# Who reads a shared PSUM bank, and in which order: opening, gates and last token tiles of a transformer layer

## The chip, the cores and the metric

The kernel runs on one core of one Trainium2 chip. The core has a matrix engine (TensorE, PE in the profile, with its weight loads as PEld), VectorE (DVE), ScalarE (ACT), GpSimd (POOL) and SyncE (SP, which here issues most of the transfers). Data move by DMA from HBM into the on-chip memory SBUF; TensorE writes its sums to PSUM, eight banks of 512 float32 columns on 128 partitions, and DVE and ACT read them there. The metric is the device time of one execution, in microseconds.

## The reference

One layer of a diffusion backbone on 512 tokens of width 1024, with 256 context tokens, batch 1, float32. What matters here:

```python
hc = modulate(rms_norm(ctx, norm1_g), sh1c, sc1c)     # sh, sc: from silu(c) @ w_ada + b_ada
s_f, s_b = context_states(hc, w_in, ...)              # k, v, gates of the context only
hx = modulate(rms_norm(x, norm1_g), sh1x, sc1x)
y_x = token_mixer(hx, ..., s_f, s_b)                  # hx @ w_in, then SGU and GLA branches, w_o
x = x + g1x * y_x
hx2 = modulate(rms_norm(x, norm2_g), sh2x, sc2x)
x = x + g2x * conv_ffn(hx2, ...)                      # 1024 -> 2 x 2816, 3x3 conv, gelu, -> 1024
return rms_norm(x, final_norm_g)
```

The token mixer's second branch is a gated linear attention (GLA) with 4 heads and two directions. Its gates are, for each direction d and head,

```python
z  = lr @ w2[d] + b2[d]                # lr: 16 columns of hx @ w_in for each direction
la = log_sigmoid(z) / 16               # computed as min(z, 0) - log(1 + exp(-|z|)), over 16
b  = cumsum(la) in chunks of 64        # then exp(b), exp(-b), exp(b_last - b) scale q and k
```

The same gates are needed for the 512 latent tokens (called x here) and for the 256 context tokens (called c).

## The kernel before

Every large product is computed as three matmuls of rounded pieces: an operand is split into a high part (a rounded copy) and a low part (the operand minus that copy), and high by high, low by high and high by low are added up in one PSUM bank. So every weight and activation costs, beside its matmuls, one cast (mostly on ACT) and one subtraction (mostly on DVE).

**Order.** The kernel is written for one core as a straight program. A scheduler that knows the tiles places semaphores between the engines; each engine then works off its instructions in the order of the program, unless a helper fixes another one. `in_order(start, engines)` chains all instructions since `start` on the engines named in the order in which they are written; it covers the opening on TensorE, ACT and DVE (from STRICT to the end of the first keys). `behind(start, name)` puts what was issued since `start` behind a named instruction. Accesses of two engines to one PSUM bank are kept apart by a semaphore, two reads too, so that the later one in program order waits for the earlier one.

**PSUM.** `mm()` and `gl()` hand out banks from two pools (mostly mm for the large products and gl for small ones); a bank asked for again waits until its last reader is done.

**Opening.** The 512 tokens are normalised, and TensorE transposes them (L585) into one bank for each block k of 128 model columns: `xps[0]` to `xps[6]` and `ps7`. `x_out` copies a bank to SBUF as xT (L590). `ada_dot(g)` computes shift and scale of a group of blocks from w_ada (tile wa, L621), DVE copies the sum to asb (L595 for the first, L768 for the rest), `ada_sel` turns it into columns (L630, L633 to L635) and `ada_mod` applies them (L642, L644) and splits the block into hxh and hxl (L374, L375). Meanwhile the loop over k adds up six banks `fps`: query and key of head 0 (gl, two banks) and the values of heads 0 and 1 for four token tiles (mm, four banks), three passes z for each k (L697). Their weights come by DMA in four pieces; `first_split(i)` splits piece i into qkh and wh on ACT (L607) and qkl and wl on DVE (L608). The dictionary `AT` says ahead of which pass z the next group's `ada_dot` stands; its `ada_sel` and `ada_mod` stand one pass later.

**Values.** After the loop each of the four value banks holds 128 tokens by 256 columns of head 0 and of head 1. `v_out` reads each half twice: ACT writes the high part (L716), DVE the low part (L717), half by half. Right behind it stand the keys of head 1 (L382) with the transposes of the context (L655, into a gl bank that ACT scales to hcf, L664).

**Heads.** Each head's gates are made by `step_z`: `step_zx` computes z of the 512 latent tokens, one bank for each direction, and `step_zc` that of the 256 context tokens, both directions in one bank of 256 columns each (L826). Of each half ACT takes the absolute value into lc (L832) and DVE the minimum with zero into mc (L833). ACT exp and ln follow (L834, L835), then DVE's running sums (`bc` for x at L875, `suf` for c at L840 and L845), and the products with q and k (L899 to L903), which TensorE transposes (L919, L927). Steps of one head run among the matmuls of other work (L401, L382) and of the head before it: L907 is the three-piece product of its outputs and states, into gl banks that DVE copies (o, L989) and ACT squares and sums (junk, L991).

**End.** The last layer product is the down projection (L1639). Token tiles 0 to 3 are finished one after the other; for each, `out_step` multiplies by the gate (yt, L1686), adds (x, L1687) and lets ACT square and sum (L1692); `out_tok` then makes the root (n3b, L1705 to L1708; ACT Sqrt, L1709; DVE reciprocal n3r, L1710), scales one half on ACT (xg, L1713, whose DMA ACT issues at L1714) and the other on DVE (L1715, whose DMA SP issues at L1716). The last tile's half is computed as 384 and 128 columns. ACT's Sqrt lies in another table of functions than what ran before; its load appears as ACT_TABLE_LOAD.

Of the kernel before, what the change touches and what calls it, by code (L numbers as in the profile page):

```python
# [16 lines left out]
P = 128  # L17
D = 1024
S = 512
LC = 256  # L20
# [13 lines left out]
def backbone_kernel(  # L34
# [58 lines left out]
    def behind(start, name):  # L93
        for i in traced()[start:]:
            tc.add_manual_dep(i, name, mybir.DependencyInfo(
                mybir.DependencyClass.NoSync, mybir.DependencyReason.DATA), reason="behind")

    ident = const([P, P], "ident")
# [505 lines left out]

    def first_split(i):
        for raw, wh, wl in (fqk[i], fv[i]):
            A.copy(wh, raw)  # L607
            V.tensor_tensor(wl, raw, wh.bitcast(F32), op=ALU.subtract)  # L608
# [28 lines left out]
    def ada_mod(g):  # L637
        k0 = G0[g]
        for k in range(k0, k0 + GROUPS[g]):
            f = fx[k]  # L640
            if k == 0:
                A.activation(f, xps[0], AF.Identity, bias=bm_[:, 0, 0:1], scale=am[:, 0, 0:1])  # L642
            else:
                V.tensor_scalar(f, f, am[:, k, 0:1], bm_[:, k, 0:1], op0=ALU.mult, op1=ALU.add)  # L644
            hx.append(split_act(f, S, "hx", eng=V.tensor_copy if k == k0 else A.copy))
            if k in (4, 6):
                first_split(k // 2)

# [60 lines left out]

    def v_out(t, ps):  # L710
        for h in range(2):
            dst = heads[h]["vx"][t // 2] if t < 4 else heads[h]["vc"]
            split_ps(*(z[:, t % 2, :] for z in dst), ps[:, h * 256:(h + 1) * 256])

    def split_ps(hi, lo, ps):
        A.copy(hi, ps)  # L716
        V.tensor_tensor(lo, ps, hi.bitcast(F32), op=ALU.subtract)  # L717
# [22 lines left out]
    x_out(2, xps[2], V.tensor_copy)  # L740
    first_split(0)
    x_out(3, xps[3], A.copy)
    x_out(4, xps[4], A.copy)
    x_out(5, xps[5], A.copy)
    x_out(6, xps[6], V.tensor_copy)
    ps7 = gl()
    for t in range(4):
        x_turn(ps7, t, KT - 1)
    x_out(KT - 1, ps7, A.copy)
    lrx = heap([96, S], F32R, s="lrx")  # L750
    fps = [gl() for _ in range(2)] + [mm() for _ in range(4)]
    AT = {0: 1, 1: 0, 2: 0, 3: 1, 4: 0}
    for k in range(KT):
        g = max(i for i in range(NG) if G0[i] <= k)
        nxt = g + 1 if k == G0[g] + GROUPS[g] - 1 and g + 1 < NG else None
        if k == 1:
            first_split(1)
        if k == 6:
# [6 lines left out]
        for z in range(3):  # L765
# [3 lines left out]
            if nxt and z == AT[g] + 1:  # L769
                ada_sel(nxt, dst)  # L770
                ada_mod(nxt)
            for i in range(6):
                if k or i > 1:
# [46 lines left out]

    def step_zc(h):
        S_ = heads[h]
        bcol, wz = gate_col(h)
# [6 lines left out]
        for d in range(2):  # L830
            zd = zc[:, d * LC:(d + 1) * LC]
            A.activation(l[:, d, :], zd, AF.Abs, bias=bcol[d])  # L832
            V.tensor_scalar(m[:, d, :], zd, bcol[d], 0.0, op0=ALU.add, op1=ALU.min)  # L833
        A.activation(l, l, AF.Exp, scale=-1.0)  # L834
# [14 lines left out]

    def step_zx(h):  # L850
        S_ = heads[h]
        bcol, wz = gate_col(h)
# [6 lines left out]
        for d in range(2):  # L859
# [4 lines left out]
            lx.append(l_)  # L864
            mx.append(m_)
        for t_ in lx:
            A.activation(t_, t_, AF.Exp, scale=-1.0)
# [3 lines left out]
        for d in range(2):  # L871
# [19 lines left out]
            S_["eq"].append(lx[d])  # L891
            S_["ek"].append(bc)
    def step_decay(h):
        S_ = heads[h]
# [14 lines left out]
    def step_z(h):  # L909
        step_zx(h)  # L910
        step_zc(h)
        step_decay(h)
# [785 lines left out]

    def out_tok(t, hf, part, before):

        b_, r = small(1, "n3b"), small(1, "n3r")
        start = len(traced())
        part()
        if before > 1:
# [4 lines left out]
        A.activation(r, ss3[:, t, before:before + 1], AF.Sqrt, bias=b_, scale=1.0 / D)  # L1709
        V.reciprocal(r, r)  # L1710
        in_order(start, V.engine)
        o = 1 - hf
        A.mul(xg[t], xg[t], r)  # L1713
        adma(out[0, t * P:(t + 1) * P, o * 512:(o + 1) * 512], xg[t])  # L1714
        V.scalar_tensor_tensor(x1[t][hf], x1[t][hf], r, fng[hf], op0=ALU.mult, op1=ALU.mult)  # L1715
        dma(out[0, t * P:(t + 1) * P, hf * 512:(hf + 1) * 512], x1[t][hf])  # L1716
# [61 lines left out]
    steps_r(r0, "p5")  # L1778
    steps_r(r1, "p5")
    for t in range(2):  # L1780
        first_half(c22[t], 1, 2 + t)
# [9 lines left out]
    for t in range(2):  # L1791
        for name, act, j in (("p1", "a12", 0), ("p5", "s4", 1)):
            for n_, i in enumerate(rbs):
                down(bank[name][t], ops[act, TAIL + n_], t, tw[i], j, False, True, again=True)
            if j == 0:
                first_half(bank[name][t], 0, t)
        out_tok(t, 1, lambda: out_step(bank["p5"][t], 1, t, 0, 512, 1), 1)
    for i, jj, p in t4s:
        down(bank["p7"][0], ops["a22", p], 0, tw[i], jj, False, True, again=True)
    out_tok(2, 0, lambda: out_step(bank["p7"][0], 0, 2, 0, 512, 1), 1)  # L1800
    for n_, (c0, n) in enumerate(((0, 384), (384, 128))):
        ps = mm()
        for i, jj, p in t4s:
            down(ps[:, :n], ops["a22", p], 1, tw[i], jj, p == TAIL, p == NP - 1, c0, n)
        step = lambda: out_step(ps[:, :n], 0, 3, c0, n, 1 + n_)
        if n_ == 0:
            step()
        else:
            out_tok(3, 0, step, 2)

# [29 lines left out]
```

## Time and profile before

| | |
|---|---|
| median of 3 runs | 929.21 us (928.75 to 931.22) |
| the profiled execution, its own time | 928.0 us |
| its span in the profile | 926.3 us |
| granted TensorE clock, mean | 0.997 |
| busy: PE, DVE, ACT, POOL | 900.1, 755.5, 483.8, 61.9 us |
| HBM read, written | 131.32 MB, 2.10 MB |

The profile is one execution; its time is 1.7 us above its span, and 1.2 us below the median. A row of the waits names the engine and line that waited, then the engine, tile and line that released it, and then the time in total, the number of such waits and the longest. A row of the timeline has the start and the duration of an instruction (or of several of one kind in a row, with their count), its line, operation, output and inputs, and in brackets how long the engine was idle ahead of it and what ended that.

### The profile page before, as it was taken

How to read it: one execution, taken by the hardware profiler on the slowest of the kernel's cores; microseconds unless marked ns; L12 is line 12 of the kernel's file. 1: busy time of each engine (PE TensorE's matmuls, PEld its weight loads, DVE VectorE, ACT ScalarE, POOL GpSimd, SP SyncE). 2: the span in 40 equal slices, each digit the busy share in tenths (PEclk: the TensorE clock that was granted, in tenths of full speed). 3: DMA queues.
4: the chain of work that ended last, by engine and by line, in shares of the span. 5: the costliest groups of instructions: out<-in, count | busy, mean ns of one | idle time of the engine just before them, and what ended most of it. 6: DMA issues, size and time to landing. Idle time of an engine off the chain costs nothing.

```text
span 926.3 us, 12858 instructions
## 1 busy us (share of the span) xinstructions
PE 900.1 (97%) x4671; PEld 754.7 (81%) x4671; DVE 755.5 (82%) x1312; ACT 483.8 (52%) x872; POOL 61.9 (7%) x90
## 2 busy tenths in 40 slices
PE   6999999999999999999999999999999999999996
PEld 5676898988878888888888877988888888888885
DVE  5567758689679878878686787899988888899997
ACT  5136546457465456757562459633333333357674
POOL 3000000000000011111111010000000000122100
PEclk9999999999999999999999999999999999999998
DMA  9940411132069474968668075344434333489632
GB/s 276 339 130 27 133 47 46 46 101 59 23 206 317 133 184 124 301 152 230 181 192 227 10 182 159 92 148 118 143 114 126 103 91 105 101 215 246 177 100 91
DMA packets 125820, 134.26 MB, mean 145 GB/s; under 512 B 7177, under 2 KB 84309, under 8 KB 125757
## 3 DMA queue, kind: packets, MB, share of 16 engines
q1 hardware_dynamic: 115357, 116.80, 40.5%
q0 software_dynamic: 8672, 15.43, 10.2%
q10 hardware_dynamic: 1728, 1.22, 0.4%
q8 instruction: 37, 0.61, 0.3%
q14 instruction: 26, 0.21, 0.1%
HBM read 131.32 MB, written 2.10 MB: 144 GB/s over the span
## 4 chain that ended last, share of the span: by engine, by line
PE 87%; DVE 5%; ACT 2%; DMA 2%; SPq 1%; issue 1%; DVEq 0%; ACTq 0%; POOLq 0%
PE mm L382 32%; PE mm L408 9%; PE gl L455 9%; PE mm L455 7%; PE gl L1639 6%; PE mm L1639 5%; PE gl L408 4%; PE gl L907 3%; PE mm L401 3%; PE mm L697 1%; PE mm L1011 1%; PE mm L393 1%; DVE bc L875 1%; SPq L319 1%; PE gl L938 1%
## 5 line engine op out<-in xcount | busy, mean ns | idle before, releaser
L143 ACT CAST wh<-raw 128x1024 fp32r<-128x1024 f32 x110 | 115.1, 1049 | 89.6 <-PE mm L382 56.5
L144 DVE TENSOR_TENSOR wl<-raw,wh 128x1024 fp32r<-128x1024 f32 x110 | 133.7, 1218 | 30.3 <-ACT wh L143 28.1
L382 PE MATMUL mm<-h2l,wh 128*128 128x512 f32 (+1 forms) x352 | 133.7, 380 | 0.0
L382 PE MATMUL mm<-h2h,wl 128*128 128x512 f32 (+1 forms) x352 | 133.6, 379 | 0.0
L382 PE MATMUL mm<-h2h,wh 128*128 128x512 f32 (+1 forms) x352 | 133.6, 379 | 0.0
L1532 DVE SCALAR_TENSOR_TENSOR cacc<-ca,ccol,cacc 128x441 f32<-128x441 f32 (+2 forms) x176 | 121.5, 693 | 4.4 <-ACT cacc L1520 0.9
L382 PEld LDWEIGHTS mm<-h2l,wh 128*128 128x128 f32 x352 | 66.2, 188 | 12.6
L382 PEld LDWEIGHTS mm<-h2h,wh 128*128 128x128 f32 x352 | 66.2, 188 | 12.5
L382 PEld LDWEIGHTS mm<-h2h,wl 128*128 128x128 f32 x352 | 66.2, 188 | 12.4
L1535 ACT ACTIVATE cacc<-cacc 128x512 f32<-128x512 f32 x22 | 13.9, 632 | 90.0 <-DVE cacc L1532 89.9
L1160 DVE SCALAR_TENSOR_TENSOR acc<-wa,cs,acc 128x512 f32<-128x512 f32 x64 | 45.5, 745 | 3.9 <-DMA wa<-in_w_ada_dram 3.9
L382 PE MATMUL mm<-hxh,wh 128*128 128x512 f32 x104 | 41.7, 401 | 0.0
L382 PE MATMUL mm<-hxh,wl 128*128 128x512 f32 x104 | 40.9, 394 | 0.0
L382 PE MATMUL mm<-hxl,wh 128*128 128x512 f32 x104 | 40.7, 392 | 0.0
L217 ACT CAST wh<-tt 128x512 fp32r<-128x512 f32 x48 | 28.4, 622 | 19.0 <-DMA tt<-in_w_in_dram 7.2
L218 DVE TENSOR_TENSOR wl<-tt,wh 128x512 fp32r<-128x512 f32 x48 | 31.7, 685 | 7.5 <-ACT wh L217 7.4
L1581 ACT CAST wh<-raw 128x1024 fp32r<-128x1024 f32 x22 | 23.0, 1052 | 17.6 <-PE mm L1639 8.5
L193 POOL DMA_DIRECT2D tt<-in_w_in_dram x24 | 20.8, 1086 | 165.8 <-DVE xl L1261 72.4
L1582 DVE TENSOR_TENSOR wl<-raw,wh 128x1024 fp32r<-128x1024 f32 x22 | 26.8, 1218 | 1.8 <-ACT wh L1581 1.7
L455 PE MATMUL mm<-wl,hxh 128*128 128x512 f32 x72 | 28.1, 391 | 0.0
L455 PE MATMUL mm<-wh,hxh 128*128 128x512 f32 x72 | 28.0, 389 | 0.0
L455 PE MATMUL mm<-wh,hxl 128*128 128x512 f32 x72 | 28.0, 389 | 0.0
(524 smaller groups left out, 2382.7 us busy)
## 6 DMA issues: line engine op xcount, KB each, us to landing
raw<-in_w_in_dram SPq DMA_DIRECT2D x54, 512.0 KB, 4.7
wa<-in_w_ada_dram SPq DMA_DIRECT2D x96, 256.0 KB, 5.1
raw<-in_ffn_w_up_dram SPq DMA_DIRECT2D x44, 512.0 KB, 4.2
raw<-in_ffn_w_down_dram SPq DMA_DIRECT2D x22, 512.0 KB, 3.5
tt<-in_w_in_dram POOLq DMA_DIRECT2D x24, 256.0 KB, 6.7
raw<-in_w_br_a_dram SPq DMA_DIRECT2D x8, 512.0 KB, 4.9
raw<-in_w_br_b_dram SPq DMA_DIRECT2D x8, 512.0 KB, 4.2
raw<-in_w_o_dram SPq DMA_DIRECT2D x8, 512.0 KB, 5.7
```

What stands on the lines that cost most here:

```text
L143: A.copy(wh, raw)
L144: V.tensor_tensor(wl, raw, wh.bitcast(F32), op=ALU.subtract)
L217: A.copy(wh[:, kk, :], tt[j][kk])
L218: V.tensor_tensor(wl[:, kk, :], tt[j][kk], wh[:, kk, :].bitcast(F32), op=ALU.subtract)
L382: T.matmul(ps, a[:, k, :], b[:, c0:c0 + n], start=(k == 0 and i == 0), stop=(k == KT - 1 and i == 2))
L401: T.matmul(ps, a[:, t * P:(t + 1) * P], b[:, k % 4, :], start=(k == 0 and i == 0), stop=(k == KT - 1 and i == 2))
L408: T.matmul(ps, a, b[:, k % 2, :], start=(k == 0 and i == 0), stop=(k == KT - 1 and i == 2))
L455: T.matmul(ps[t], a, b[:, kk, :], start=(first and i == 0), stop=(j == 1 and kk == 1 and i == 2), skip_group_check=again)
L907: T.matmul(ps, p_, q_, start=(start and z == 0), stop=(stop and z == 2))
L1160: V.scalar_tensor_tensor(a_, w_, cs[:, k, 0:1], a_, op0=ALU.mult, op1=ALU.add)
L1532: V.scalar_tensor_tensor(o, a_[:, r0 + dy:r1 + dy, c0 + dx:c1 + dx], wcol(tap), o, op0=ALU.mult, op1=ALU.add)
L1639: T.matmul(ps, a[:, t * P:(t + 1) * P], w[b][:, j, c0:c0 + n], start=(first and i == 0), stop=(last and i == 2), skip_group_check=again)
```

## The change

Five places are written in another way. What is computed stays the same; no product, copy or transfer is added or taken away.

1. Opening: `first_split` is cut into `first_high` (ACT) and `first_low` (DVE). `first_low(0)` stands behind the copies of blocks 6 and 7, and block 6 (DVE) and 7 (ACT) are copied ahead of block 5; `ps7` comes from the mm pool; `first_low(1)` stands behind `ada_mod` of block 2; and the `ada_dot` of the next group during block 2 moves from pass 0 to pass 1.
2. Values: `v_out` has both high parts of a bank on ACT first, then both low parts on DVE.
3. Gates: `step_z` has the heads of x and c (matmuls, Abs, minimum) first and then their tails; in the context's head both Abs come first and then both minima.
4. End: the root, the first and the last half of each tile are separate functions, and from tile 1 on all DVE and ACT instructions keep the order in which they are written.
5. ACT's table for Sqrt is loaded after the preparation of the last down operands, by a `preload_act_table`.

```diff
+    def table_for(func):
+        name = [i.name for i in traced() if i.engine == nc.scalar.engine][-1]
+        start = len(traced())
+        A.preload_act_table(func)
+        behind(start, name)
...
     def v_out(t, ps):
+        dst = [[z[:, t % 2, :] for z in (heads[h]["vx"][t // 2] if t < 4 else heads[h]["vc"])] for h in range(2)]
         for h in range(2):
-            dst = heads[h]["vx"][t // 2] if t < 4 else heads[h]["vc"]
-            split_ps(*(z[:, t % 2, :] for z in dst), ps[:, h * 256:(h + 1) * 256])
+            A.copy(dst[h][0], ps[:, h * 256:(h + 1) * 256])
+        for h in range(2):
+            V.tensor_tensor(dst[h][1], ps[:, h * 256:(h + 1) * 256], dst[h][0].bitcast(F32), op=ALU.subtract)
...
     x_out(2, xps[2], V.tensor_copy)
-    first_split(0)
+    first_high(0)
     x_out(3, xps[3], A.copy)
     x_out(4, xps[4], A.copy)
-    x_out(5, xps[5], A.copy)
-    x_out(6, xps[6], V.tensor_copy)
-    ps7 = gl()
+    ps7 = mm()
     for t in range(4):
         x_turn(ps7, t, KT - 1)
     x_out(KT - 1, ps7, A.copy)
+    x_out(6, xps[6], V.tensor_copy)
+    first_low(0)
+    x_out(5, xps[5], A.copy)
...
-    AT = {0: 1, 1: 0, 2: 0, 3: 1, 4: 0}
+    AT = {0: 1, 1: 0, 2: 1, 3: 1, 4: 0}
...
         if k == 1:
-            first_split(1)
+            first_high(1)
...
                 ada_mod(nxt)
+                if k == 1:
+                    first_low(1)
...
         for d in range(2):
-            zd = zc[:, d * LC:(d + 1) * LC]
-            A.activation(l[:, d, :], zd, AF.Abs, bias=bcol[d])
-            V.tensor_scalar(m[:, d, :], zd, bcol[d], 0.0, op0=ALU.add, op1=ALU.min)
+            A.activation(l[:, d, :], zc[:, d * LC:(d + 1) * LC], AF.Abs, bias=bcol[d])
+        for d in range(2):
+            V.tensor_scalar(m[:, d, :], zc[:, d * LC:(d + 1) * LC], bcol[d], 0.0, op0=ALU.add, op1=ALU.min)
...
     def step_z(h):
-        step_zx(h)
-        step_zc(h)
+        zx_head(h)
+        zc_head(h)
+        zx_tail(h)
+        zc_tail(h)
         step_decay(h)
...
+    table_for(AF.Sqrt)
...
-        out_tok(t, 1, lambda: out_step(bank["p5"][t], 1, t, 0, 512, 1), 1)
+        start = len(traced())
+        out_step(bank["p5"][t], 1, t, 0, 512, 1)
+        out_root(t, 1)
+        V.reciprocal(root[t], root[t])
+        if t == 0:
+            out_first(t, 1)
+            out_last(t, 1)
     for i, jj, p in t4s:
         down(bank["p7"][0], ops["a22", p], 0, tw[i], jj, False, True, again=True)
-    out_tok(2, 0, lambda: out_step(bank["p7"][0], 0, 2, 0, 512, 1), 1)
+    out_step(bank["p7"][0], 0, 2, 0, 512, 1)
+    out_root(2, 1)
+    out_first(1, 1)
     for n_, (c0, n) in enumerate(((0, 384), (384, 128))):
...
-        step = lambda: out_step(ps[:, :n], 0, 3, c0, n, 1 + n_)
-        if n_ == 0:
-            step()
-        else:
-            out_tok(3, 0, step, 2)
+        out_step(ps[:, :n], 0, 3, c0, n, 1 + n_)
+    out_last(1, 1)
+    V.reciprocal(root[2], root[2])
+    out_root(3, 2)
+    out_first(2, 0)
+    out_last(2, 0)
+    V.reciprocal(root[3], root[3])
+    out_first(3, 0)
+    out_last(3, 0)
+    in_order(start, V.engine, A.engine)
```

On three places the order of instructions moves as follows (line numbers of each kernel's own file; a name's number tells one tile from another).

DVE in the opening, from the split of block 0 to the split of block 1, before:

```order
L375 TENSOR_TENSOR hxl_417<-xT_270,hxh_416 128x512
L590 COPY xT_272<-mm_265 128x512
L608 TENSOR_TENSOR qkl_140<-qkraw_136,qkh_139 128x512
L608 TENSOR_TENSOR wl_115<-raw_113,wh_114 128x1024
L590 COPY xT_276<-gl_269 128x512
L768 COPY asb_467<-gl_450 128x128
L633 TENSOR_TENSOR am<-gl_473,bsc_256 128x2
...
L375 TENSOR_TENSOR hxl_480<-xT_271,hxh_479 128x512
L608 TENSOR_TENSOR qkl_162<-qkraw_158,qkh_161 128x512
L608 TENSOR_TENSOR wl_118<-raw_116,wh_117 128x1024
L768 COPY asb_510<-gl_493 128x128
```

The same stretch in the changed kernel:

```order
L381 TENSOR_TENSOR hxl_417<-xT_270,hxh_416 128x512
L596 COPY xT_272<-mm_265 128x512
L596 COPY xT_276<-gl_269 128x512
L617 TENSOR_TENSOR qkl_140<-qkraw_136,qkh_139 128x512
L617 TENSOR_TENSOR wl_115<-raw_113,wh_114 128x1024
L781 COPY asb_467<-gl_450 128x128
L642 TENSOR_TENSOR am<-gl_473,bsc_256 128x2
...
L381 TENSOR_TENSOR hxl_480<-xT_271,hxh_479 128x512
L781 COPY asb_508<-gl_491 128x128
L642 TENSOR_TENSOR am<-gl_516,bsc_256 128x2
```

The copy of block 6 (xT_276) went ahead of the low parts of piece 0, and the copy of block 2's sums (asb) no longer stands behind the low parts of piece 1.

DVE around the gates of head 1, from the copies of head 0's outputs to the products with q and k, before:

```order
L989 COPY o_1102<-gl_1581 128x256
L875 SCALAR_TENSOR_TENSOR bc_1464<-mx_1454,lx_1452 128x128 x4
L875 SCALAR_TENSOR_TENSOR bc_1477<-mx_1458,lx_1456 128x128
L879 TENSOR_TENSOR dec_1469<-bc_1464 128x4
...
L875 SCALAR_TENSOR_TENSOR bc_1477<-mx_1458,lx_1456 128x128 x3
L833 TENSOR_SCALAR mc_1494<-gl_1490,vec_b 128x256
...
L833 TENSOR_SCALAR mc_1494<-gl_1490,vec_b 128x256
...
L903 TENSOR_TENSOR lc_1493<-lc_1493,kc_1128 128x512
L989 COPY o_1101<-gl_1621 128x256
```

The same stretch in the changed kernel:

```order
L1025 COPY o_1102<-gl_1581 128x256
L729 TENSOR_TENSOR vx_1406<-mm_1594,vx_1405 128x256
L1025 COPY o_1101<-gl_1621 128x256
L852 TENSOR_SCALAR mc_1464<-gl_1460,vec_b 128x256 x2
L908 SCALAR_TENSOR_TENSOR bc_1473<-mx_1454,lx_1452 128x128 x4
L908 SCALAR_TENSOR_TENSOR bc_1486<-mx_1458,lx_1456 128x128
L912 TENSOR_TENSOR dec_1478<-bc_1473 128x4
...
L908 SCALAR_TENSOR_TENSOR bc_1486<-mx_1458,lx_1456 128x128 x3
...
L937 TENSOR_TENSOR lc_1463<-lc_1463,kc_1128 128x512
```

Both minima of the context (mc), one low part of the values and one copy of an output now stand ahead of the running sums (bc, printed as SCALAR_TENSOR_TENSOR).

DVE at the end, from tile 1's sum to tile 2's root, before:

```order
L1687 TENSOR_TENSOR x_1154_5486<-x_1154_5486,yt_8785 128x512
L1708 TENSOR_SCALAR n3b_8783<-ss_7837 128x1
L1686 TENSOR_TENSOR yt_8807<-mm_7842,g_1439_7391 128x512
L1687 TENSOR_TENSOR x_1155_5488<-x_1155_5488,yt_8807 128x512
L1710 RECIPROCAL n3r_8784<-n3r_8784 128x1
L1708 TENSOR_SCALAR n3b_8805<-ss_7837 128x1
```

The same stretch in the changed kernel:

```order
L1723 TENSOR_TENSOR x_1154_5486<-x_1154_5486,yt_8784 128x512
L1744 TENSOR_SCALAR n3b_8788<-ss_7837 128x1
L1839 RECIPROCAL n3r_8789<-n3r_8789 128x1
L1722 TENSOR_TENSOR yt_8802<-mm_7842,g_1439_7391 128x512
L1723 TENSOR_TENSOR x_1155_5488<-x_1155_5488,yt_8802 128x512
L1744 TENSOR_SCALAR n3b_8806<-ss_7837 128x1
```

Tile 1's reciprocal (n3r) now stands ahead of the two steps of tile 2 (yt and x). In the values the order on each engine is the old one; what moved there are the semaphores between ACT and DVE.

More of the change, by code (lines that the diff above doesn't have):

```diff
@@ L603, in backbone_kernel, with first_high, first_low @@
     am, bm_ = const([P, KT, 2], "am"), const([P, KT, 2], "bm")
-    def first_split(i):
+    def first_high(i):
+        for raw, wh, _ in (fqk[i], fv[i]):
+            A.copy(wh, raw)
+    def first_low(i):
         for raw, wh, wl in (fqk[i], fv[i]):
-            A.copy(wh, raw)
             V.tensor_tensor(wl, raw, wh.bitcast(F32), op=ALU.subtract)
@@ L646, in ada_mod @@
             if k in (4, 6):
-                first_split(k // 2)
+                first_high(k // 2)
+                first_low(k // 2)
     def ctx_turn(k2):
@@ L821, in step_zc, with zc_head @@
     def step_zc(h):
+        zc_head(h)
+        zc_tail(h)
+    def zc_head(h):
         S_ = heads[h]
@@ L830, in step_zc, with zc_tail @@
         for d in range(2):
-            zd = zc[:, d * LC:(d + 1) * LC]
-            A.activation(l[:, d, :], zd, AF.Abs, bias=bcol[d])
-            V.tensor_scalar(m[:, d, :], zd, bcol[d], 0.0, op0=ALU.add, op1=ALU.min)
+            A.activation(l[:, d, :], zc[:, d * LC:(d + 1) * LC], AF.Abs, bias=bcol[d])
+        for d in range(2):
+            V.tensor_scalar(m[:, d, :], zc[:, d * LC:(d + 1) * LC], bcol[d], 0.0, op0=ALU.add, op1=ALU.min)
+        S_["zc"] = l, m
+    def zc_tail(h):
+        S_ = heads[h]
+        l, m = S_.pop("zc")
         A.activation(l, l, AF.Exp, scale=-1.0)
@@ L850, in step_zx, with zx_head @@
     def step_zx(h):
+        zx_head(h)
+        zx_tail(h)
+    def zx_head(h):
         S_ = heads[h]
@@ L865, in step_zx, with zx_tail @@
             mx.append(m_)
+        S_["zx"] = lx, mx
+    def zx_tail(h):
+        S_ = heads[h]
+        lx, mx = S_.pop("zx")
         for t_ in lx:
@@ L909, in step_z @@
     def step_z(h):
-        step_zx(h)
-        step_zc(h)
+        zx_head(h)
+        zc_head(h)
+        zx_tail(h)
+        zc_tail(h)
         step_decay(h)
@@ L1697, in first_half, with out_root @@
         V.tensor_tensor(xg[t], x1[t][hf], fng[hf], op=ALU.mult)
-    def out_tok(t, hf, part, before):
+    root = {}
+    def out_root(t, before):
         b_, r = small(1, "n3b"), small(1, "n3r")
-        start = len(traced())
-        part()
         if before > 1:
@@ L1709, in out_tok, with out_first, out_last @@
         A.activation(r, ss3[:, t, before:before + 1], AF.Sqrt, bias=b_, scale=1.0 / D)
[L1710 to L1715, printed above, removed]
+        root[t] = r
+    def out_first(t, hf):
+        A.mul(xg[t], xg[t], root[t])
+        adma(out[0, t * P:(t + 1) * P, (1 - hf) * 512:(2 - hf) * 512], xg[t])
+    def out_last(t, hf):
+        V.scalar_tensor_tensor(x1[t][hf], x1[t][hf], root[t], fng[hf], op0=ALU.mult, op1=ALU.mult)
         dma(out[0, t * P:(t + 1) * P, hf * 512:(hf + 1) * 512], x1[t][hf])
```

## The prediction

> **What bounds the kernel now.** I read the busy shares first, then the stretches, then what TensorE waited for.
>
> ```profile
> span 926.3 us, 12858 instructions
> PE 900.1 (97%) x4671; PEld 754.7 (81%) x4671; DVE 755.5 (82%) x1312; ACT 483.8 (52%) x872; POOL 61.9 (7%) x90
> 225.00:540.00 315.00, 314.97 (x1489) 262.19 (x1488) 251.98 (x397) 177.25 (x309) 32.13 (x39) 1.00 0.62 174
> 585.00:905.00 320.00, 320.00 (x1449) 266.50 (x1449) 294.02 (x429) 146.35 (x212) 18.79 (x22) 1.00 0.49 136
> ```
>
> TensorE sets the time. In the two long stretches (the first figure after the length is its busy time) it never stops, and its clock is full (1.00). None of the edits touches them, and they make what comes before them count in full: whatever TensorE saves ahead of 225 us arrives at the end, because nothing there waits for anything that starts on its own. So only a wait of TensorE's, or the last microseconds after its last matmul, can be gained or lost. Its waits, longest first, as far as the edits reach them:
>
> ```profile
> PE gl L630 <- DVE asb L768: 1.9, 1, 1.9
> PE gl L697 <- ACT xT L590: 1.9, 1, 1.9
> PE gl L655 <- ACT hcf L664: 1.7, 1, 1.7
> PE gl L907 <- DVE mc L833: 1.6, 2, 0.8
> PE gl L907 <- ACT junk L991: 0.3, 1, 0.3
> PE gl L919 <- DVE lc L903: 0.2, 1, 0.2
> ```
>
> Two lie in the opening, one in the values, three in the gates. They add up to 1.9 + 1.9 + 1.7 + 1.6 + 0.3 + 0.2 = 7.6 us: the most that can be gained at the start, if nothing new is waited for.
>
> **Opening.** These rows are TensorE's, ACT's and DVE's timelines from 18 to 34 us.
>
> ```profile
> 20.57 0.50 PE L697 MATMUL gl<-hxh,qkh 128*128 128x512 f32 x1 [1.89 <-ACT xT L590]
> 30.75 0.39 PE L630 MATMUL gl<-selm,asb 128*128 128x4 f32 x2 [1.93 <-DVE asb L768]
> 19.91 1.09 ACT L590 COPY xT<-gl 128x512 f32<-128x512 f32 x2
> 27.67 0.62 ACT L607 CAST qkh<-qkraw 128x512 fp32r<-128x512 f32 x1 [6.66 <-DMA wa<-in_w_ada_dram]
> 28.20 1.04 ACT L607 CAST wh<-raw 128x1024 fp32r<-128x1024 f32 x1
> 29.27 1.23 DVE L608 TENSOR_TENSOR wl<-raw,wh 128x1024 fp32r<-128x1024 f32 x1 [0.26 <-ACT wh L607]
> 30.41 0.28 DVE L768 COPY asb<-gl 128x128 f32<-128x128 f32 x1
> 18.00:30.00 12.00, 8.72 (x90) 6.12 (x90) 7.46 (x15) 4.58 (x8) 0.00 (x0) 1.00 1.18 302
> ```
>
> The first wait: the second query and key matmul needs a gl bank, and it gets the one whose transposes ACT copies out last but one (block 5, in the pair at 19.91). In the change that bank is no longer the one that the key sum gets, since ps7 moves to the mm pool and blocks 6 and 7 are copied first. The second wait: DVE has to finish wl of piece 1 (29.27 + 1.23 = 30.50) before it copies asb; wl waits for ACT's two casts, and these for a transfer that lands at 27.67. TensorE had nothing to do from 28.82 on. In the change the copy of asb stands ahead of these low parts, and needs only TensorE's own product.
>
> What is late next? wl of piece 1 is needed at the first pass of block 2 that uses it, and the cast wh ends at 28.20 + 1.04 = 29.24, so its low parts (0.69 + 1.23 from rows of the same form) end at about 31.2 even behind the new copies; block 2 begins at about 30.5 with the passes that need only qkh and wh. Nothing waits there. The second wait goes whole: 1.93 of idle time and about 0.15 of refilling the pipeline, 2.1 us.
>
> The first wait can't go whole. The next value matmuls want the bank of ps7, which ACT copies at about 20.0 to 20.5 now, and the products of w_ada behind it want a transfer while DMA is at 1.18 of its engines' time at 302 GB/s: 1 MB of w_ada takes 3.4 us at that rate. An earlier TensorE meets these transfers closer to their landing. The bounds are nothing and 2.1 us; I take 1.3, nearer the upper end, because no row shows TensorE waiting for w_ada after 18 us. **Opening: −3.4 us, from −1.5 to −4.0.**
>
> **Values.** ACT's, DVE's and TensorE's timelines from 69 to 75 us:
>
> ```profile
> 67.38 0.36 ACT L716 CAST vx<-mm 128x256 fp32r<-128x256 f32 x1
> 70.45 0.65 ACT L716 CAST vx<-mm 128x256 fp32r<-128x256 f32 x2 [0.55 <-DVE vx L717]
> 72.84 0.37 ACT L716 CAST vx<-mm 128x256 fp32r<-128x256 f32 x1 [0.55 <-DVE vx L717]
> 73.11 2.86 ACT L664 ACTIVATE hcf<-gl,bm,am 128x256 f32<-128x256 f32 x6
> 72.05 0.76 DVE L717 TENSOR_TENSOR vx<-mm,vx 128x256 fp32r<-128x256 f32 x2 [0.44 <-ACT vx L716]
> 74.19 0.66 PE L655 MATMUL gl<-ident,xin 128*128 128x128 f32 x4 [1.72 <-ACT hcf L664]
> ```
>
> ACT and DVE hand each bank to and fro: high part of head 0, low part, high part of head 1, low part. ACT starts a pair every 1.2 us and idles 0.55 in each. Its hcf, which stands behind the last high part at 73.11, is what TensorE's second round of transposes waits for. With both highs first, ACT goes to the next bank at once; at 0.27 us from start to start (73.11 − 72.84) eight casts take 2.2 us instead of the 5.8 from 67.38 to 73.21. They end near 69.7, and hcf starts over 3 us sooner. TensorE's own work reaches L655 at 72.47 (74.19 − 1.72), and the two hcf activations that free its bank then end at about 70.7. The wait goes with its refill, 1.9 us. DVE's eight lows (0.35 us apart within the pair at 72.05, from 68.8 on) end at 71.6, some 2 us sooner, so the hch and hcl behind them don't become the new wait. About 0.2 us of small waits behind, where the next vx lows and the context's low-rank part met the same hand-over, go too. **Values: −2.1 us, from −1.7 to −2.4.**
>
> [...] The two engines never overlap on a bank in these rows. [...]
>
> **Gates of heads 1 to 3.** The rows are of head 1; heads 2 and 3 look alike.
>
> ```profile
> 143.59 0.51 PE L907 MATMUL gl<-st,qh 128*128 128x256 f32 x2 [0.80 <-DVE mc L833]
> 138.88 0.47 ACT L832 ACTIVATE lc<-gl,vec_b 128x256 f32<-128x256 f32 x1 [0.23 <-PE gl L907]
> 142.37 0.47 ACT L832 ACTIVATE lc<-gl,vec_b 128x256 f32<-128x256 f32 x1 [0.23 <-DVE mc L833]
> 138.52 1.69 DVE L875 TENSOR_TENSOR_SCAN bc<-mx,lx 128x128 f32<-128x128 f32 x5 [2.69 <-PE gl L907]
> 141.88 0.46 DVE L833 TENSOR_SCALAR mc<-gl,vec_b 128x256 f32<-128x256 f32 x1
> 143.07 0.47 DVE L833 TENSOR_SCALAR mc<-gl,vec_b 128x256 f32<-128x256 f32 x1
> 147.45 0.68 DVE L903 TENSOR_TENSOR lc<-lc,kc 128x512 f32<-128x512 f32 x1
> 148.19 0.66 PE L919 MATMUL gl<-ident,lc 128*128 128x128 f32 x4
> ```
>
> Gain: zc's bank is read by Abs, minimum, Abs, minimum, the last at 143.07 behind DVE's running sums, and the L907 that wants this bank waits 0.80 (0.96 with the refill). With both Abs first (138.9 to 139.7) and the minima ahead of the running sums, the bank is free at about 140.6, some 3 us before it is wanted, though L907 too moves forward there. Over three heads: 0.96 + 0.96 + 0.42 = 2.3 us (1.6 and 0.3 of waits, and refills).
>
> Loss: DVE works in order. Its running sums now stand behind two minima, which stand behind two Abs, whose lc is a piece of memory that an L907 releases at about 138.5, and behind a copy of an output. The running sums start at about 140.4 rather than 138.52, while the minima (0.8 us for two) are only moved. So 1.9 − 0.8 − 0.2 (what DVE idled around them) leaves lc's product (L903) about 0.8 us later, ready at 148.95 instead of 148.13. TensorE is rid of the 0.96, but four more of the neighbouring 512-column matmuls (0.23 us each) stand ahead of L919 in the new order, so it comes there at about 148.0 as before, and meets a wait of 1.0 us: what is gained at L907 is given back here. Behind it some banks wait for ACT's junk rows, which now stand behind the later suf products: another 0.3 to 0.5 us. Head 1 comes out at +0.3, head 2 at +0.1, head 3 at +0.4, where both output copies stand ahead of the minima. **Gates: +0.8 us, from −2.0 to +2.0.**
>
> **End.** Timelines of DVE, ACT and SP after 911 us, and TensorE's last stretch:
>
> ```profile
> 915.89 0.69 DVE L1686 TENSOR_TENSOR yt<-mm,g 128x512 f32<-128x512 f32 x1
> 917.23 0.15 DVE L1710 RECIPROCAL n3r<-n3r 128x1 f32<-128x1 f32 x1
> 921.54 0.75 DVE L1715 SCALAR_TENSOR_TENSOR x<-x,n3r,fng 128x512 f32<-128x512 f32 x1
> 911.98 1.28 ACT L1709 ACT_TABLE_LOAD   x1
> 915.91 0.63 ACT L1692 ACTIVATE yt<-x 128x512 f32<-128x512 f32 x1 [1.11 <-DVE x L1687]
> 916.67 0.29 ACT L1709 ACTIVATE n3r<-ss,n3b 128x1 f32<-128x1 f32 x1
> 921.54 0.72 ACT L1713 ACTIVATE xg<-xg,n3r 128x512 f32<-128x512 f32 x1 [0.23 <-DVE n3r L1710]
> ```
>
> The table load (1.28) goes to about 879 us, where ACT has 0.6 to 1.1 us idle between its tasks and 146 of 320 us busy in all; it is hidden. Out of the end it shortens only tile 0's root, and DVE did other work meanwhile (tile 1's yt and x), so it is worth nothing at the last instruction.
>
> The written order puts tile 1's reciprocal ahead of tile 2's yt. The root that it inverts ends at 916.67 + 0.29 = 916.96, so DVE stands from 915.89 to about 917.0, and tile 2's yt, which had its sum, starts at 917.1 rather than 915.89: 1.2 us later. Some of that comes back, since DVE idled 0.47 us before its last reciprocal and two scalings now stand behind the small pieces. I count the new order through with the durations above: last scaling on DVE at 922.3 rather than 921.54, on ACT at 922.5 rather than 921.54. Four output transfers then leave within about 1.1 us, where before pairs left 2 us apart; each is 256 KB. So the last landing moves by 0.8 plus a few tenths. **End: +1.0 us, from −0.3 to +1.5.** If the root came before DVE got there, the lower bound would hold.
>
> **Sum.** −3.4 − 2.1 + 0.8 + 1.0 = −3.7 us. On the profiled execution's 928.0 that is 924.3; that one lies 1.2 us below the median of the runs (929.21), and as a change of the median the sum gives **925.5 us**. With the terms' own bounds this case reaches from about 923.5 to 927.5.
>
> **Rivals.**
>
> *The transfers take the opening's gain.* DMA is at its limit there (1.18 of its time), and the split of piece 1 waited for a landing. If w_ada for the next blocks lands late, TensorE waits for it in place of asb; the opening gives only its lower bound of 1.5. Against it: no wait on w_ada in the rows. Then −1.5 − 2.1 + 0.8 + 1.0 = −1.8, 927.4 us: within the noise.
>
> *The gates pay in full.* If lc's memory is free earlier than I count, the minima end before the x products are wanted, the running sums start on time and all 2.3 us of L907 go; and the in-order end costs nothing. −3.4 − 2.1 − 2.3 + 0.3 = −7.5, 921.7 us. For it: DVE idled 2.69 us before its sums at 138.52. Against it: that idle time ended with an L907, and the minima need one as well.
>
> *DVE's queue turns the gates into the bound: slower.* If the minima can't start until zc's matmuls have come in their old place behind L401 (zc's first Abs in the second half at 142.37 shows how late that could be), the running sums start at 143.2 instead of 138.5. That is 4.7 late, less the 0.8 moved, and L919 waits about 3.9 us in each of three heads: +11.7 in place of +0.8, 936 us. It decides from 2.4 us a head on: the other terms give −4.5, and 3 x 2.4 is 7.2, which makes the kernel 2.7 slower. For it: DVE is a strict queue and nothing else can be done behind a waiting minimum. Against it: the first Abs ran at 138.88 already.
>
> *The change doesn't do what it says.* The waits are put down to the last semaphore; if banks are handed out otherwise than I read it, the second query and key matmul waits for another copy and only wl's wait goes. −2.1 + 0.8 + 1.0 and nothing from the values gives −0.3, 928.9 us.
>
> **Chances.** The forecast 0.52, transfers 0.19, gates in full 0.13, the queue 0.09, no effect 0.07. A measurement of this kernel tells 0.3% (2.8 us) from no change, so faster begins below 926.4. Of the forecast's 0.52 about 0.42 lies below it; with 0.13 and 0.02 of the transfers' case: faster 0.57, same 0.34, slower 0.09. The range holds the forecast, the transfers and the upper half of the gates' case: 922.0 to 929.0 us.
>
> **What would show it.** Right: no wait of L630 on asb near 30 us and no wait of L655 on hcf; the transposes now at 74.19 near 68.9 (3.4 and 1.9 earlier); ACT's casts of vx in pairs 0.27 us apart without the 0.55; L907 no longer waiting for mc, but L919 for lc by about 1 us; DVE idle for about 1.1 us before tile 1's reciprocal; the last output scaling about 0.8 us later after the last matmul than now. Wrong: a wait on a DMA of wa in the opening; running sums that start with no idle time before them; a TensorE stop behind 225 us that takes back what was won.

## The result, and the profile after

The changed kernel takes 926.19 us (median of 6 runs, 925.15 to 927.03), the kernel before 930.54 us in the same comparison (6 runs, 928.75 to 931.88). The ratio is 0.9952 with a 95% interval of 0.9939 to 0.9964: 4.4 us faster, between 3.4 and 5.7. The forecast was 3.7 us faster.

The profiled execution of the changed kernel took 927.03 us, that of before 928.0 us, only 1.0 us more. Both kernels stream the same number of columns through TensorE, in nearly the same order, so I compared when the same number had been streamed (by adding up the columns of all matmuls in each trace). That tells where the changed kernel is ahead, in microseconds:

| at this time of the kernel before | 15 | 46 | 67 | 82 | 136 | 236 | 380 | 430 | 590 | 917 |
|---|---|---|---|---|---|---|---|---|---|---|
| changed kernel ahead by | 0.05 | 3.63 | 3.63 | 5.58 | 5.47 | 5.48 | 5.46 | 2.43 | 2.09 | 2.09 |

The opening gives 3.57 (15 to 46 us), the values 1.95 (67 to 82), the gates nothing (136 to 236). Then 3.03 us are lost between 380 and 430 us, where no edit lies. The waits of TensorE in the changed kernel, longest first, of the lines that matter here:

```profile
span 925.3 us, 12858 instructions
...
PE gl L955 <- DVE lc L937: 2.4, 2, 1.2
...
PE gl L955 <- ACT wh L149: 1.1, 1, 1.1
...
PE mm L461 <- DVE wl L150: 0.8, 1, 0.8
PE gl L461 <- DVE es L491: 0.6, 1, 0.6
PE gl L845 <- DVE lrc L683: 0.6, 1, 0.6
PE mm L461 <- ACT wh L149: 0.6, 1, 0.6
```

The four rows of the prediction's list with 1.9, 1.9, 1.7 and 1.6 us are gone. L955 (the transposes of lc, L919 before) now waits 3.5 us in three heads, and three rows of L461 (L455 before) make up 2.0 us of the loss behind 380 us. The same 45 us as a stretch, before and then changed (after the length: PE's busy time):

```profile
380.00:425.00 45.00, 45.00 (x199) 36.99 (x198) 38.46 (x52) 26.98 (x42) 6.93 (x8) 1.00 0.82 223
```

```profile
380.00:425.00 45.00, 42.97 (x186) 34.24 (x185) 38.23 (x51) 25.87 (x40) 8.46 (x11) 1.00 0.80 214
```

Whether that loss belongs to the change was the first question for the experiments. The opening, on ACT, TensorE and DVE of the changed kernel:

```profile
18.91 1.56 ACT L596 COPY xT<-mm 128x512 f32<-128x512 f32 x3
...
19.48 1.54 PE L707 MATMUL mm<-wh,hxh 128*128 128x512 f32 x4
...
25.85 0.29 DVE L781 COPY asb<-gl 128x128 f32<-128x128 f32 x1 [0.34 <-PE gl L630]
...
27.75 0.62 ACT L613 CAST qkh<-qkraw 128x512 fp32r<-128x512 f32 x1 [6.79 <-DMA wa<-in_w_ada_dram]
```

The copy of asb now ends 1.6 us before the casts that the transfer holds up. Four value matmuls take 1.54 us from 19.48 on, where before they took 1.08 (from 21.38): the last of them starts at 20.52, right behind the last of ACT's three copies (18.91 + 1.56 = 20.47).

The values, on ACT and TensorE of the changed kernel:

```profile
63.75 2.28 ACT L723 CAST vx<-mm 128x256 fp32r<-128x256 f32 x8
65.86 1.10 ACT L674 ACTIVATE hcf<-gl,bm,am 128x256 f32<-128x256 f32 x2
...
68.68 0.60 PE L665 MATMUL gl<-ident,xin 128*128 128x128 f32 x4
```

Eight casts in 2.28 us with no idle time between them, hcf right behind, and the transposes that waited 1.72 us at 74.19 start at 68.68 without a wait.

The gates of head 1, on ACT, DVE and TensorE:

```profile
133.07 0.84 ACT L850 ACTIVATE lc<-gl,vec_b 128x256 f32<-128x256 f32 x2
...
134.22 0.87 DVE L852 TENSOR_SCALAR mc<-gl,vec_b 128x256 f32<-128x256 f32 x2
135.01 1.68 DVE L908 TENSOR_TENSOR_SCAN bc<-mx,lx 128x128 f32<-128x128 f32 x5
...
142.76 0.69 DVE L937 TENSOR_TENSOR lc<-lc,kc 128x512 f32<-128x512 f32 x1
...
143.60 0.63 PE L955 MATMUL gl<-ident,lc 128*128 128x128 f32 x4 [1.08 <-ACT wh L149]
```

The kernel is 5.47 us ahead here, so the running sums at 135.01 are at 140.48 in the time of before, where they stood at 138.52: 1.96 us later. They start right behind the minima, with no idle time ahead of them. The product lc ends at 143.45, before at 148.13 − 5.47 = 142.66: 0.8 later. L955 follows that end by 0.15 us; the row names a cast on ACT, but it is lc that ends just ahead of it, and in the other two heads the row names lc.

The end, on DVE, ACT and TensorE:

```profile
914.85 0.17 DVE L1839 RECIPROCAL n3r<-n3r 128x1 f32<-128x1 f32 x1 [1.05 <-ACT n3r L1745]
914.93 0.67 DVE L1722 TENSOR_TENSOR yt<-mm,g 128x512 f32<-128x512 f32 x1
...
920.22 0.75 DVE L1753 SCALAR_TENSOR_TENSOR x<-x,n3r,fng 128x512 f32<-128x512 f32 x1
...
920.86 0.72 ACT L1749 ACTIVATE xg<-xg,n3r 128x512 f32<-128x512 f32 x1 [0.41 <-ACT xg L1749]
...
916.02 0.28 PE L1675 MATMUL mm<-wh,ol 128*128 128x128 f32 x1
```

DVE idles 1.05 us ahead of tile 1's reciprocal. On DVE the last scaling comes where the prediction counted it (920.22 + 2.1 = 922.3 in the time of before), on ACT 0.5 us later than counted (920.86 + 2.1 = 923.0 for 922.5). From the start of the last matmul to the end of the span it takes 925.3 − 916.02 = 9.3 us, before 926.3 − 918.12 = 8.2 us.

### The profile page after: what moved, and what is told of

The parts are those of the page before. It is cut to its first block, busy times and chain, and to the rows that moved or that the text cites. A ratio compares the mean times of both kernels' runs of the same rounds, so it can differ in the third digit from the quotient of the medians.

```text
span 925.3 us, 12858 instructions
## 1 busy us (share of the span) xinstructions
PE 900.3 (97%) x4671; PEld 754.8 (82%) x4671; DVE 755.1 (82%) x1312; ACT 484.8 (52%) x872; POOL 61.9 (7%) x90
## 4 chain that ended last, share of the span: by engine, by line
PE 84%; DVE 7%; DMA 4%; ACT 3%; issue 2%; ACTq 0%; POOL 0%; SPq 0%; DVEq 0%; POOLq 0%
PE mm L388 32%; PE mm L414 10%; PE gl L1675 6%; PE gl L461 4%; PE mm L1675 4%; PE mm L461 4%; PE gl L414 4%; PE gl L941 3%; PE mm L707 2%; PE mm L407 2%; DMA tt<-in_w_in_dram 2%; PE gl L707 1%; PE mm L1047 1%; DVE bc L908 1%; PE mm L399 1%
## 5 line engine op out<-in xcount | busy, mean ns | idle before, releaser
L461 PE MATMUL mm<-wl,hxh 128*128 128x512 f32 x72 | 28.1, 391 | 0.8 <-DVE wl L150 0.8
L461 PE MATMUL mm<-wh,hxh 128*128 128x512 f32 x72 | 28.1, 391 | 0.6 <-ACT wh L149 0.6
L461 PE MATMUL mm<-wh,hxl 128*128 128x512 f32 x72 | 28.0, 389 | 0.0
```

Source lines behind the costliest of these rows:

```text
L461: T.matmul(ps[t], a, b[:, kk, :], start=(first and i == 0), stop=(j == 1 and kk == 1 and i == 2), skip_group_check=again)
```

## The experiments

My theory was the prediction's sum with the sizes that the trace now showed: opening −3.6, values −1.9, gates 0, end +1.1. The rivals were that transfers or later waits take part of it back, and that the loss behind 380 us comes with the edits.

### Each part alone

Opening alone (the changed kernel's opening in the kernel before):

```diff
+    ps7 = mm()
...
+    x_out(KT - 1, ps7, A.copy)
+    x_out(6, xps[6], V.tensor_copy)
+    first_low(0)
+    x_out(5, xps[5], A.copy)
...
+                if k == 1:
+                    first_low(1)
```

> The opening's edits alone (low parts behind, blocks 6 and 7 copied ahead of block 5, ps7 from the other pool, the product of w_ada a pass later). My theory: both waits of TensorE go, its matmuls behind 40 us start 3.6 us earlier, and the kernel is 3 to 4 us faster (ratio 0.9965 to 0.996). Rival, the transfers take it: a wait on wa appears and 1.5 us are left (0.9984). Rival, the stretch of 390 to 420 us stands on transfers that don't come earlier: TensorE is 3.6 us ahead at 380 us and about 2.4 us ahead at 480 us (0.9975).

Measured: ratio 0.9955 (0.9939 to 0.9971), 4.2 us faster. TensorE gains 3.61 us between 15 and 46 us of the time of before, and no row of it waits for a transfer of wa. It loses 1.89 us between 380 and 430 us.

Values alone:

```diff
         for h in range(2):
+            A.copy(dst[h][0], ps[:, h * 256:(h + 1) * 256])
+        for h in range(2):
+            V.tensor_tensor(dst[h][1], ps[:, h * 256:(h + 1) * 256], dst[h][0].bitcast(F32), op=ALU.subtract)
```

> Only v_out is changed: both high parts of a bank on ACT, then both low parts on DVE. My theory: the wait of L655 on hcf (1.72 us) goes with its refill, TensorE is 1.9 us ahead from 76 us on, and the kernel is 1.9 us faster (ratio 0.998). Rival, DVE's low parts become the new wait: less than 0.5 us is gained. Rival, the stretch of 390 to 420 us stands on transfers: as little as this gain would pass it whole.

Measured: 0.998 (0.9967 to 0.9993), 1.9 us faster, with 1.95 us gained between 67 and 82 us, the same as in the changed kernel to the second digit.

Gates alone:

```diff
     def step_z(h):
-        step_zx(h)
-        step_zc(h)
+        zx_head(h)
+        zc_head(h)
+        zx_tail(h)
+        zc_tail(h)
```

> Only the gates' steps are regrouped (heads of x and c first, then their tails; both Abs, then both minima). My theory: L907 loses its wait on mc (0.96 us for each of heads 1 and 2, 0.4 for head 3), the transposes of lc take it back (0.8 to 1.0 in each), and the sum is between -0.3 and +0.8 us (ratio 1.000 to 1.001). Rival, the gates pay in full: -2.3 us (0.9975). Rival, the queue of DVE becomes the bound: over +2.4 us a head (1.008 and more).

Measured: 1.0001 (0.9988 to 1.0015). Between 100 and 236 us TensorE is 0.05 us earlier in all: L907's waits on mc (1.6 us) are gone, and the transposes of lc wait 3.5 us in their place. The idle time of TensorE there grew from 2.25 to 3.50 us, and its busy time shrank by 1.30: the length of a wait isn't what it costs.

End alone, with the table's load:

```diff
+        V.reciprocal(root[t], root[t])
+        if t == 0:
+            out_first(t, 1)
+            out_last(t, 1)
...
+    in_order(start, V.engine, A.engine)
```

> Only the end: the written order of DVE and ACT from tile 1 on and the earlier load of the table. My theory: TensorE's last matmul stays where it was, DVE idles about 1.1 us ahead of tile 1's reciprocal, and the end lies 1.0 us later (ratio 1.001). Rival, the order costs nothing: 0.0 (1.000). Rival, the table's load on the way to the last root counts: -0.5 to -1.3 us (0.999).

Measured: 1.0006 (0.9995 to 1.0017). In its profile 9.29 us lie between the last matmul and the end, as in the changed kernel, and 8.18 to 8.22 in every kernel with the old end. The load of the table left no trace in the time: with it, and with one reciprocal in another place (below), the end takes 8.20 us, as without it.

The four ratios add up to −4.2 − 1.9 + 0.1 + 0.6 = −5.4 us, the change itself measured −4.4; the intervals of the parts are over 1 us wide each, so the two agree. What the parts also showed is that the loss behind 380 us is there in kernels that change nothing ahead of it: the kernel with only another end lost 1.97 us between 380 and 430 us.

### The kernel before once more

> The kernel before, profiled once more. My theory: its first profile was a fortunate one. A second shows what the kernels with an untouched stretch showed: TensorE waits of 1 to 2.5 us between 385 and 420 us on wh, wl and es, and in the opening either a lower granted clock behind the wait on xT or a wait on asb of about 3 us. Rival, the waits between 385 and 420 us come with the edits: then it has none.

This execution took 932.77 us, and TensorE lost 3.17 us between 380 and 430 us against the first profile of the same program. Its stretch and its waits:

```profile
380.00:425.00 45.00, 42.58 (x185) 34.17 (x185) 38.26 (x53) 27.43 (x44) 6.94 (x8) 1.00 0.80 217
```

```profile
PE gl L455 <- DVE es L485: 1.7, 2, 1.0
...
PE mm L455 <- DVE wl L144: 0.8, 1, 0.8
```

So the loss doesn't come with the edits. Of the twelve further profiles it is absent in one (the last kernel below) and lies between 0.66 and 3.17 us in eleven. The changed kernel's chain of waits goes there through transfers, with casts on ACT and low parts on DVE between them; three of its pieces are these (start, length, what).

```profile
377.27 6.35 DMA tt<-in_w_in_dram
386.16 9.94 DMA tt<-in_w_in_dram
403.49 7.24 DMA raw<-in_w_in_dram
```

Put on the time of the kernel before, four pieces of tt are issued between 362.6 and 366.3 us, at the same times within 0.02 us in all thirteen profiles. A load of raw that follows is issued at 372.2 to 372.5 us in the three that lose least (0 to 0.66 us) and at 373.0 to 375.4 us in the other ten. So at least part of the lateness arises between these two. What makes it differ from one execution to another, no run here tells.

### The opening's two halves

Only the low parts of piece 1 moved:

```diff
         if k == 1:
-            first_split(1)
+            first_high(1)
...
                 ada_mod(nxt)
+                if k == 1:
+                    first_low(1)
```

> Of the opening's edits one alone: the low parts of piece 1 stand behind the copy of the next group's sums (asb) and its scaling. My theory: the wait of L630 on asb near 30 us goes whole and the other wait (on xT, 1.89 us) stays. In the kernels whose opening is untouched that wait was 0.2, 0.6, 1.9 and 3.0 us long in one profile each, so it is worth 1.4 us on the mean: ratio 0.998 to 0.999. Rival, the gain hangs on all edits together: the wait moves to another row, and nothing is gained.

Measured: 0.998 (0.9962 to 0.9999), 1.9 us faster. The wait on asb is gone.

Only the banks and copies of blocks 5 to 7 moved, and the low parts of piece 0:

```diff
-    x_out(5, xps[5], A.copy)
-    x_out(6, xps[6], V.tensor_copy)
-    ps7 = gl()
+    ps7 = mm()
...
+    x_out(6, xps[6], V.tensor_copy)
+    first_low(0)
+    x_out(5, xps[5], A.copy)
```

> Of the opening's edits the others but the pass of w_ada's product: blocks 6 and 7 copied ahead of block 5, the low parts of piece 0 behind them, ps7 from the mm pool. My theory: the wait of L697 on xT goes (1.9 us) and 1.3 to 2.1 us reach 40 us, unless the wait on asb grows by as much, since it ends with a transfer: then TensorE is earlier at 25 us and not at 40 us, and the ratio is 1.000. With the first 0.998.

Measured: 1.0019 (1.0005 to 1.0033): slower by 1.8 us. The wait on xT is gone, and TensorE is ahead by 1.15 us at 26 us. But the wait on asb has grown. Its rows on ACT, DVE and TensorE:

```profile
28.27 0.62 ACT L607 CAST qkh<-qkraw 128x512 fp32r<-128x512 f32 x1 [7.03 <-DMA wa<-in_w_ada_dram]
...
31.01 0.28 DVE L774 COPY asb<-gl 128x128 f32<-128x128 f32 x1
...
31.34 0.39 PE L633 MATMUL gl<-selm,asb 128*128 128x4 f32 x2 [3.27 <-DVE asb L774]
```

The copy of asb is pinned (it stands behind low parts whose casts wait for a transfer, so it can't come before the transfer lands); an earlier TensorE only waits longer. And the wait costs more than its length. The stretches behind it (the third figure from the end is the granted clock):

```profile
33.00:36.00 3.00, 3.00 (x15) 1.90 (x18) 0.93 (x2) 0.00 (x0) 0.00 (x0) 0.51 1.09 357
36.00:39.00 3.00, 3.00 (x41) 2.49 (x34) 0.39 (x2) 0.00 (x0) 0.00 (x0) 0.92 1.10 344
```

Behind that wait of 3.27 us TensorE's granted clock was 0.51 from 33 to 36 us and 0.92 from 36 to 39; in the first profile of the kernel before, behind its wait of 1.93 us, it was 1.00 in both. So the halves don't add up: the one is worth 1.9 us, the other costs 1.8, and together with the later product of w_ada they are worth 4.2. The rows say why: the banks pay once the copy of asb no longer hangs on the transfer. What share the later product of w_ada has, no run separates.

### What sets the pace in the gates

The changed kernel, with the product that makes lc ahead of those that make lx:

```diff
             V.tensor_tensor(S_["ek"][d], v4(kx), S_["ek"][d], op=ALU.mult)
-            V.tensor_tensor(S_["eq"][d], v4(qx), S_["eq"][d], op=ALU.mult)
             S_["k"].append(S_["ek"][d])
-            S_["q"].append(S_["eq"][d])
         V.tensor_tensor(S_["ec"], S_["ec"], kc.unsqueeze(1).to_broadcast([P, 2, LC]), op=ALU.mult)
+        for d in range(2):
+            V.tensor_tensor(S_["eq"][d], v4(qx), S_["eq"][d], op=ALU.mult)
+            S_["q"].append(S_["eq"][d])
```

> The changed kernel, with the product that makes lc (for the context) issued ahead of the two products that make lx, so that it stands one 0.6 us step earlier on DVE. My theory: behind the regrouped gates DVE is the bound; L955's wait in heads 1 to 3 ends with its queue, and each loses 0.6 us: -1.8 us in all against the changed kernel by 230 us. Rival, L955 waits for banks that ACT reads (its junk and wh rows): the waits stay as they are, 0.0.

Measured: 0.9955 (0.9941 to 0.9968), no different from the changed kernel, and 0.17 us later between 100 and 236 us. The scheduler moved lc one step ahead on DVE, but in head 1 it also moved the transposes of lc three matmuls ahead on TensorE (three times 0.23 us), so TensorE came earlier by as much as lc did:

```profile
PE gl L956 <- DVE lc L935: 3.2, 3, 1.2
```

All three waits now name lc as what was waited for, which settles that it is DVE's product and not ACT's rows. The size was missed (no gain where 1.8 us was expected), because I had taken the order on TensorE as fixed.

### The end, and the best version

The end's edits alone, with tile 1's reciprocal behind tile 2's two steps:

```diff
-        V.reciprocal(root[t], root[t])
         if t == 0:
+            V.reciprocal(root[t], root[t])
             out_first(t, 1)
...
+    V.reciprocal(root[1], root[1])
     out_root(2, 1)
```

> The end's edits alone, with one difference: tile 1's reciprocal stands behind tile 2's yt and x rather than ahead of them. My theory: the wait ahead of that reciprocal (1.05 us) is what the written order costs, so the time from TensorE's last matmul to the end falls from 9.29 us to 7.8 to 8.3 (8.18 before). Rival, it is the bunching of the last transfers: it stays above 9.

Measured: 1.0002 (0.9987 to 1.0018), and 8.20 us from the last matmul to the end. The reciprocal's place costs the 1.1 us, not the bunching of the transfers. The written order without it brings nothing over the old end (8.18).

The same line moved in the changed kernel:

> The changed kernel with one line moved: tile 1's reciprocal behind tile 2's yt and x. My theory: the end falls from 9.29 to 8.20 us behind the last matmul, and the kernel is 1.1 us faster than the changed one (ratio to before 0.994, where the changed one had 0.9952). Rival, the end's time hides behind the last transfers: no difference.

Measured: 924.26 us, 0.9925 (0.9907 to 0.9944); 8.18 us at the end. DVE in it:

```profile
915.18 0.69 DVE L1723 TENSOR_TENSOR x<-x,yt 128x512 f32<-128x512 f32 x1
915.79 0.15 DVE L1846 RECIPROCAL n3r<-n3r 128x1 f32<-128x1 f32 x1
```

There is no idle time ahead of the reciprocal. In this execution L630 waited 0.7 us for wa, and the opening gave 2.7 us instead of 3.6: the rival on transfers in its smallest form.

The same with the old gates as well (the change's diff in the gates undone):

> As the kernel of the same call that moves tile 1's reciprocal, but with the old gates (one step after the other, Abs and minimum alternating). My theory: DVE's work up to lc sets TensorE's pace there in either order, so the two kernels agree within 0.3 us at 230 us, with waits of L907 on mc in this one and waits on lc in the other. Rival, the regrouping alone is worth up to 2 us: this one is slower by as much.

Measured: 924.46 us, 0.9924 (0.9906 to 0.9942), the same. At 236 us its TensorE is 5.33 us ahead of before, of which the gates (100 to 236 us) change nothing (0.01), with the old wait in its old place:

```profile
138.26 0.50 PE L922 MATMUL gl<-st,qh 128*128 128x256 f32 x2 [0.80 <-DVE mc L848]
```

These two beat the kernel before by 6.8 and 6.6 us. By their medians they lie 1.9 and 1.7 us under the change, but they ran beside other runs of the kernel before, and their intervals touch the change's: that they beat the change is likely, not shown, beyond the 1.1 us that the profile shows at the end.

## Why the prediction was right

**The direction and the sum were right**: −3.7 us forecast, −4.4 measured; 925.5 us forecast, 926.19 in runs beside which the kernel before took 930.54 rather than 929.21.

**Opening, −3.4.** The trace shows −3.57, made up as forecast: 1.4 us by 26 us from the first wait and 2.2 more by 36 us from the second. That the first wait can't go whole held, and by the first of the two reasons given: the value matmuls wait for ACT's copies. The other, the transfers of w_ada, holds nothing up in this profile. What I had not seen is that its gain hangs on the second edit, by the pinned transfer, and that the kernel before is not always held up as in its first profile. In four of its six profiles with an untouched opening the clock fell behind the first wait (to 0.53 to 0.74 as the mean from 21 to 24 us); these lost 1.5 us by it (one 2.8), and got 1.3 to 1.8 of that back by 36 us, because their wait on asb shrank to 0.6 us or less. Over the six, TensorE's 15-to-46 us stretch took 0.3 us less to 2.7 us more than in the first one, 0.5 more on the mean, so the edits are worth more on the mean (3.9 us, from five profiles with the edited opening) than against the profile that I argued from.

**Values, −2.1.** Measured −1.95 in the stretch, −1.9 alone. ACT's eight casts took 2.28 us where I had 2.2. The refill that the forecast counts with a wait is in the rows of before: the matmul ahead of the wait on hcf started at 72.08 and the one behind it at 74.19, and of these 2.11 us 1.72 were idle and 0.23 are what such a matmul takes from start to start, so 0.16 are left. The 0.2 us of small waits behind did not come; L845 now waits 0.6 for lrc where it waited 0.2.

**Gates, +0.8.** The step was mis-sized: it measured 0.0. Gain and loss came as worked out (1.06 gained at L907 in head 1 and 0.97 given back at the transposes of lc; 0.97 and 0.82 in head 2; the running sums 1.96 us later where I had 1.9, lc 0.8 later where I had 0.8). The further 0.3 to 0.5 us a head for banks behind ACT's junk rows did not come.

**End, +1.0.** Measured +1.1, by the wait that was named: 1.05 us of idle time ahead of the reciprocal where I had 1.1. The table's load was hidden, as forecast.

**What was wrong**: the sentence that nothing behind 225 us "waits for anything that starts on its own". Between 380 and 430 us TensorE hangs on a chain of transfers, casts and low parts that runs up to 3.2 us late, in an execution of the same program. The first profile of before showed none of it, by luck, and I took one execution's row for the rule. On the median it should cancel, since profiles of both kernels have it; between the two profiled executions it hid 3.0 of 4.4 us.

Two of the prediction's signs of being wrong appeared, and neither meant what it was meant to. The stop behind 225 us took back 3.0 us in this profile, but the kernel before has it too. The running sums of head 1 start with no idle time before them; but with the minima right ahead of them, as the forecast itself counted, they had to, so that sign could tell nothing. The size tells: the sums came 1.96 us late, where the forecast had 1.9 and the rival on DVE's queue 4.7.

**The rivals.** Transfers taking the opening's gain: seen once, 1 us of it; that DMA was at its limit there, at 302 GB/s, no run shows, and in the same profile it moved 357 GB/s from 33 to 36 us. Gates in full: no. The queue of DVE as the bound: it is the bound, but it takes back only what was won. No effect: no; the banks are what TensorE waited for.

## What to carry to other kernels

Before removing a wait, look for something pinned to a transfer behind it: moved alone, the copies and banks of the opening made this kernel 1.8 us slower, and with the low parts out of the way (and a product of w_ada a pass later) 4.2 us faster. Where one engine's queue set the pace (DVE from the running sums to lc), regrouping moved TensorE's wait from one line to another (1.6 us on mc gone, 3.5 us on lc instead) and left the time within 0.05 us. In an order written out by hand, an instruction that waits for another engine's chain belongs behind the work that is ready: one reciprocal in the wrong place cost 1.1 us.

## What the runs showed that I had not expected

TensorE's granted clock fell to 0.50 behind some waits of 1.9 us. In the opening with only the low parts moved, its row and the stretches from 21 us are:

```profile
21.40 0.80 PE L701 MATMUL gl<-hxh,qkh 128*128 128x512 f32 x1 [1.90 <-ACT xT L590]
```

```profile
21.00:24.00 3.00, 2.60 (x6) 2.13 (x7) 1.56 (x2) 0.84 (x2) 0.00 (x0) 0.50 1.19 291
24.00:27.00 3.00, 3.00 (x41) 2.10 (x41) 0.36 (x2) 0.00 (x0) 0.00 (x0) 0.94 1.14 329
```

Of the seven profiles with that wait on xT (1.9 us long in each), five show the lower clock behind it and two, the first of before among them, don't; both waits of 3.0 and 3.3 us on asb show it (0.59 and 0.51 from 33 to 36 us). In the records of all thirteen profiles the granted clock changes only at steps of 3.41 us, and these don't lie at the same place against the kernel: a step falls 0.8 us behind the start of the wait on xT in two of the seven profiles and 1.3 to 2.2 us behind it in the other five. Behind the wait on xT the lower clock lasted one step in four of the five, in which TensorE fell back by 1.4 to 1.5 us from 20 to 26 us (against the first profile of before), and two steps in the fifth (2.8 us).

In these seven, where the wait falls against the steps decided it. In the five, the step just ahead of the drop held 1.9 to 2.6 us of idle time (most of the wait on xT, and the wait of 0.69 us ahead of it). In the two others the wait was split over two steps, and neither held more than 1.5 us. Over all the profiles, from the first full clock on, the clock fell behind no step with less than 1.55 us of idle time and behind every one with more than 1.74 (idle time by TensorE's records, whose ends are modelled).

The second thing is how far one program's executions differ in where they lose time: between two profiles of the kernel before, the same stretch of 50 us differs by 3.17 us, with the same instructions.
